# A two-layer backbone step: first products of two early feed-forward tiles taken ahead, and another rule for high priority

## The chip, the cores and the metric

The kernel runs on one core of a Trainium2 chip. The metric is the device time of one execution in microseconds, and what is given for a kernel is the median of its runs. The kernel before stands at 2413.62 us (three runs, 2412.04 to 2421.06).

## The reference

640 tokens (512 latent, 128 context) of width 1024 pass two layers. A layer is a half-step feed-forward, a mixer, and a second half-step feed-forward; each of the three is wrapped in an RMS normalisation before and after, with shift, scale and gate from a conditioning vector. The mixer is a two-dimensional Fourier transform between two projections in layer 0, and 16-head attention in layer 1.

```python
def _swiglu(h, w1, w2):
    gate, up = jnp.split(h @ w1, 2, axis=-1)      # D_FF = 2816
    return (jax.nn.silu(gate) * up) @ w2

def _half_ffn(x, m, k, g_pre, g_post, w1, w2):
    h = _modulated_prenorm(x, g_pre, m, k)
    return x + 0.5 * m[:, 3 * k + 2, None] * _rmsnorm(_swiglu(h, w1, w2), g_post)
```

## The kernel before, in words

**Sub-layers and halves.** The six sub-layers n = 0 to 5 are feed-forward, mixer, feed-forward, twice; 1 (Fourier) and 4 (attention) are mixers, 0, 2, 3 and 5 feed-forward. Activations lie with channels on the partitions, 8 chunks of 128 channels by 640 tokens, and the tokens are worked in two halves of 320. Everything is float32 with split operands: a number is a high part and a low part, and a product is three matmuls, high weight by high activation (L215), high weight by low activation (L216) and low weight by high activation (L217), in `mm3`. The high part of weights is an ACT copy (L198) and the low part a DVE subtraction (L200) in `send`; of activations L209 and L210 in `split`.

**The first projection of a feed-forward** has 22 tiles f of 128 hidden columns, each with a gate and an up column block. It runs a scheme with seven products in place of eight over the two halves of the tokens and the two halves of the channels. Of the activations B11, B12 (first four chunks, halves 0 and 1) and B21, B22 (last four) it needs T1 = B12 - B11, T2 = B22 - T1, T3 = B22 - B12 and T4 = T2 - B21, made in `combine` (L481, subtractions L491). Of the weights it needs, beside gate and up, the sums that `send` makes on DVE (L182 three times, L186 once) from two raw tiles; the units of weights are called "gate", "up", "sums" and "mix". Raw tiles come by DMA from SP (L161) into four buffers, the sums taking one of them; there are six high and six low weight buffers. `unit(i)` sends units up to three ahead of the one that is used.

**The start of a feed-forward.** `head` (L553) works half 0 alone: gate and up of tile 0 and gate of tiles 1 to 7, with B11 and B21, and keeps the sums in SBUF blocks of a ring of 20. `second` (L583) adds half 1 to tile 0: 24 matmuls with T1, then 24 with B22, then the adds L596, silu L579, product L580. `body(f)` (L599) runs a tile's other products; for tiles 1 to 7 these are mix by T1, sums by T2, sums by T3, up by T4 and, in `rest` (L639), mix by B22, with the DVE steps L615, L618, L627, L631, L632, L642 and L644 between. `w2` is the second projection in five slices (evicted on ACT at L677). `plan_ffn` (L699) writes down the order of these steps and of the weight units.

**Chains.** When a half of a sub-layer is done, `boundary` launches its `chain`: `post` normalises the output and adds it to the stream, `pre` normalises the stream for the next sub-layer (`inverse_rms` with small matmuls L430 and L438, a DVE step L432 and a POOL step L433 between; multiplications L462, scale and shift L468 and L470, then `split`, or `combine` for half 1 of a feed-forward). `tick` lets a chain go on by one step as matmuls are written. `step` gives a step of half 1 high priority, so that it goes ahead of other work that is ready on its engine, once half 0's own `post` is through (`self.normed[0][0]`).

## Time and profile before

| | before |
|---|---|
| median of three runs, us | 2413.62 (2412.04 to 2421.06) |
| the profiled execution, us | 2421.95 |
| its span, us | 2420.2 |
| mean granted TensorE clock | 0.986 |
| PE busy, us | 2325.5 (96%) |
| DVE busy, us | 1858.0 (77%) |
| ACT busy, us | 1256.2 (52%) |

The span goes from the first to the last instruction. Busy times are sums over an engine's instructions in the span; matmuls are pipelined, so that the length of one matmul in a timeline (0.31 us) is longer than the distance from one to the next. The granted clock is a share of full speed: 1.00 is the upper level, 0.50 the lower.

### The profile page before, as it was taken

What the parts mean: (1) busy time and instruction counts of PE and PEld (TensorE: products, weight loads), DVE (VectorE), ACT (ScalarE), POOL (GpSimd) and SP (SyncE); (2) the same over time, 40 slices, a digit from 0 to 9 for tenths busy, and PEclk for the clock granted to TensorE, in tenths of its full rate; (3) what the DMA queues carried; (4) which work ended last, traced back from release to release, by engine and by line L of the source; (5) the groups of instructions that cost most, each with busy time, mean ns of one, the idle gap of its engine ahead of it and who ended that gap; (6) DMA issues with size and microseconds to landing.
All of it is one profiled execution on the core that took longest, in us unless ns stands there. A gap on an engine that the chain in (4) does not pass through costs nothing.

```text
span 2420.2 us, 39323 instructions
## 1 busy us (share of the span) xinstructions
PE 2325.5 (96%) x15452; PEld 2239.1 (93%) x15452; DVE 1858.0 (77%) x3317; ACT 1256.2 (52%) x2405; POOL 72.5 (3%) x58
## 2 busy tenths in 40 slices
PE   6799999998999999999999999989999999999997
PEld 5799999997989999999899999987878898999997
DVE  7988888579788888858888887567777588675573
ACT  3554454564555554457555454744445574554544
POOL 3100000000000000000000000000000000000000
PEclk9899999999999999999999999999999999999999
DMA  6234544334424453443354353314334233332231
GB/s 255 86 123 123 174 124 125 136 94 142 143 87 146 125 168 116 137 147 114 97 157 133 121 168 119 127 56 125 123 107 129 64 112 97 95 99 66 81 124 60
DMA packets 84174, 291.77 MB, mean 121 GB/s; under 512 B 9234, under 2 KB 15634, under 8 KB 83988
## 3 DMA queue, kind: packets, MB, share of 16 engines
q1 hardware_dynamic: 83716, 288.93, 37.5%
q8 instruction: 121, 1.98, 0.3%
q14 instruction: 65, 0.53, 0.1%
q10 hardware_dynamic: 272, 0.33, 0.0%
HBM read 277.68 MB, written 11.53 MB: 120 GB/s over the span
## 4 chain that ended last, share of the span: by engine, by line
PE 75%; DVE 13%; DMA 5%; ACT 3%; issue 3%; POOL 0%; SPq 0%; DVEq 0%; ACTq 0%; POOLq 0%
PE main L215 21%; PE main L216 21%; PE main L217 21%; DMA raw<-in_w 4%; DVE lo L200 3%; DVE junk L358 3%; PE sum L1105 2%; PE score L215 2%; PE score L217 2%; PE score L216 2%; ACT hi L198 2%; DVE ring L210 1%; PE turn L1092 1%; PE score L1079 1%; DVE y L462 1%
## 5 line engine op out<-in xcount | busy, mean ns | idle before, releaser
L215 PE MATMUL main<-ring,hi 128*128 128x320 f32 x4032 | 1257.2, 314 | 35.6 <-ACT ring L209 19.0
L216 PE MATMUL main<-ring,hi 128*128 128x320 f32 x4032 | 1257.6, 312 | 7.9 <-DVE ring L210 7.5
L217 PE MATMUL main<-ring,lo 128*128 128x320 f32 x4032 | 1253.7, 312 | 7.8 <-DVE lo L200 6.0
L215 PEld LDWEIGHTS main<-ring,hi 128*128 128x128 f32 x4032 | 760.7, 189 | 52.4 <-ACT ring L209 22.8
L216 PEld LDWEIGHTS main<-ring,hi 128*128 128x128 f32 x4032 | 763.3, 189 | 15.1 <-DVE ring L210 11.3
L217 PEld LDWEIGHTS main<-ring,lo 128*128 128x128 f32 x4032 | 762.7, 189 | 11.9 <-DVE lo L200 6.8
L198 ACT ACTIVATE hi<-raw 128x1024 fp32r<-128x1024 f32 (+1 forms) x386 | 371.9, 966 | 511.9 <-PE main L216 342.1
L200 DVE TENSOR_TENSOR lo<-raw,hi 128x1024 fp32r<-128x1024 f32 (+1 forms) x380 | 419.1, 1103 | 145.5 <-ACT hi L198 142.7
L358 DVE SCALAR_TENSOR_TENSOR junk<-raw,wide 128x1024 bf16<-128x1024 f32 x256 | 312.2, 1220 | 15.0 <-DMA raw<-in_w_mod_t 11.9
L677 ACT ACTIVATE y<-main 128x320 f32<-128x320 f32 x320 | 136.7, 433 | 170.6 <-PE main L217 169.4
L665 ACT ACTIVATE main<-y 128x320 f32<-128x320 f32 x256 | 111.2, 439 | 41.1 <-DVE left L642 25.6
L394 DVE TENSOR_TENSOR total<-total,square 128x640 f32<-128x640 f32 x71 | 60.2, 853 | 86.4 <-ACT square L393 85.6
L200 DVE TENSOR_TENSOR lo<-sums,hi 128x1024 fp32r<-128x1024 f32 x84 | 102.5, 1221 | 22.1 <-ACT hi L198 21.8
L198 ACT ACTIVATE hi<-sums 128x1024 fp32r<-128x1024 f32 x84 | 88.8, 1057 | 36.9 <-PE main L216 18.2
L215 PE MATMUL score<-ring,hi 128*128 128x320 f32 x336 | 104.6, 311 | 1.2 <-ACT hi L198 1.2
L217 PE MATMUL score<-ring,lo 128*128 128x320 f32 x336 | 104.2, 310 | 0.0
L216 PE MATMUL score<-ring,hi 128*128 128x320 f32 x336 | 104.2, 310 | 0.0
L182 DVE TENSOR_TENSOR sums<-raw,raw 128x512 f32<-128x512 f32 x84 | 57.9, 689 | 40.1 <-DMA raw<-in_w 35.5
L433 POOL TENSOR_TENSOR col<-col,power 128x3 f32<-128x3 f32 x24 | 26.0, 1083 | 2081.7 <-DVE col L432 2081.7
L1094 ACT ACTIVATE right<-turn 128x384 f32<-128x384 f32 (+1 forms) x80 | 35.8, 448 | 84.3 <-PE turn L1092 83.9
L215 PEld LDWEIGHTS score<-ring,hi 128*128 128x128 f32 x336 | 63.5, 189 | 2.0 <-ACT hi L198 2.0
L618 DVE TENSOR_TENSOR left<-left,main 128x320 f32<-128x320 f32 x84 | 40.7, 485 | 30.8 <-PE main L217 29.8
(188 smaller groups left out, 2762.8 us busy)
## 6 DMA issues: line engine op xcount, KB each, us to landing
raw<-in_w SPq DMA_DIRECT2D x292, 512.0 KB, 3.6
raw<-in_w_mod_t SPq DMA_DIRECT2D x128, 512.0 KB, 3.8
raw<-in_qkv SPq DMA_DIRECT2D x26, 512.0 KB, 3.7
spill<-ring SPq DMA_DIRECT2D x12, 640.0 KB, 4.7
ring<-spill SPq DMA_DIRECT2D x12, 640.0 KB, 6.4
raw<-in_bias SPq DMA_DIRECT2D x16, 448.0 KB, 3.4
first<-in_w_mod_t SPq DMA_DIRECT2D x8, 512.0 KB, 10.2
raw<-in_four_in SPq DMA_DIRECT2D x8, 512.0 KB, 4.6
```

Source lines behind the costliest of these rows:

```text
L182: add = lambda out, a, b: nc.vector.tensor_tensor(out, a, b, op=ALU.add)
L198: nc.scalar.activation(hi, raw[:, at], AF.Copy)
L200: engine.tensor_tensor(lo, raw[:, at], hi.bitcast(F32), op=ALU.subtract)
L215: mm(out, whi, xhi, start=start, stop=False)
L216: mm(out, whi, xlo, start=False, stop=False)
L217: self.latest = mm(out, wlo, xhi, start=False, stop=stop)
L358: last = self.nc.vector.scalar_tensor_tensor(out=self.junk, in0=raw, scalar=1.0, in1=self.wide[:, cond, :], op0=ALU.mult, op1=ALU.mult, ac ...
L394: nc.vector.tensor_tensor(acc, acc, sq, op=ALU.add)
L618: tt(a, q, z, op=ALU.subtract)
L665: nc.scalar.activation(ps[:, :HALF], self.y[:, m, lo:hi], AF.Copy)
L677: nc.scalar.activation(self.y[:, m, lo:hi], ps[:, :HALF], AF.Copy)
L1105: nc.tensor.matmul(o, cache_v[:, ds] if k is None else v[:, k, ds], ptb[:, i * P + at : i * P + at + nq], start=n == 0, stop=n == len(tile ...
```

## The change

Four edits. (1) Of tiles 1 and 2 (`ACROSS`) the two mix products, by T1 and by B22, run right behind tile 0, in a new step `across`: both go into one PSUM bank, and ACT copies the bank to an SBUF block after each, so the copies hold mix by T1 and the sum of both; `body` and `rest` of these tiles read the copies in place of a bank. (2) `combine` splits B22 ahead of T2, T3 and T4, where it was last. (3) The weight units of tile 2 are listed so that its mix unit stands ahead of its sums; the order of the units comes out as before. (4) A step of half 1's chain has high priority if the chain leads into a feed-forward, from the start of the chain, and never if it leads into a mixer.

```diff
@@ -43,6 +43,7 @@
 PE_AT = (0, 2, 3, 5)
 SLICES = ((0, 2), (2, 6), (6, 11), (11, 16), (16, 22))
 EARLY = ((1, 2), (3, 4), (5, 6, 7))
+ACROSS = (1, 2)
 LATE = (NF - 2, NF - 1)
 BEHIND = (28, 20, 28, 28, 24, 0)
 BANKS = {"main": 4, "score": 2, "turn": 1, "sum": 1}
@@ -135,6 +136,7 @@
         self.normed = [[True, True], [True, True]]
         self.woven = []
         self.latest = None
+        self.hurry = False
         self.xs = {}
         self.hs = {n: Hidden(self.ring, n % 3 != 1) for n in range(DEPTH * 3)}
         self.fast = {}
@@ -229,7 +231,7 @@
 
     def step(self, half):
         due, gen = self.side[half]
-        with self.tc.high_priority() if half and self.normed[0][0] else ExitStack():
+        with self.tc.high_priority() if half and self.hurry else ExitStack():
             wait = next(gen, None)
         self.side[half] = None if wait is None else (max(due, 0) + wait, gen)
 
@@ -498,10 +500,10 @@
             put(1, h.steps[k][0], b12, b11)
         else:
             t1, t2 = h.steps[k]
+            self.split(h.at(0, c, 1, 2), h.at(1, c, 1, 2), b22)
             put(2, t2, b22, t1)
             put(3, t1, b22, b12)
             put(4, t2, t2, b21)
-            self.split(h.at(0, c, 1, 2), h.at(1, c, 1, 2), b22)
 
     def post(self, layer, sub, half, acc, last):
 
@@ -532,7 +534,7 @@
 
         nc = self.nc
         n = layer * 3 + 2 * which
-        g, kept = {}, {}
+        g, kept, crossed = {}, {}, {}
         h, high = self.h, self.tc.high_priority
         tt = nc.vector.tensor_tensor
 
@@ -596,15 +598,27 @@
                     tt(c, ps, c, op=ALU.add)
             gated(0, *kept[0], 1)
 
+        def across(f):
+
+            if "more" not in kept:
+                kept["more"] = self.ring(F32).rearrange("p (c t) -> p c t", c=4)
+            w = self.bank()[:, :HALF]
+            c = crossed[f] = [kept["more"][:, (f - 1) * 2 + i, :] for i in range(2)]
+            for i, x in enumerate((lambda k: h.sum(1, k), lambda k: h.chunk(4 + k, 1))):
+                product(w, f, "mix", 512 * i, x, not i)
+                with high():
+                    nc.scalar.activation(c[i], w, AF.Copy)
+
         def body(f):
             g[f] = self.ring(F32R).rearrange("p (a t) -> p a t", a=2)
             late, ready = f in LATE, f in kept
             x, y, z, w = (self.bank(kind)[:, :HALF] if want else None for kind, want in
-                          (("main", not ready), ("score", True), ("main", True), ("main", not late)))
+                          (("main", not ready), ("score", True), ("main", True), ("main", not late and f not in crossed)))
             q, a = (self.temp("left")[:, :HALF] for _ in range(2))
             if ready:
                 c1, s = kept[f]
-                product(w, f, "mix", 0, lambda k: h.sum(1, k), True)
+                if f not in crossed:
+                    product(w, f, "mix", 0, lambda k: h.sum(1, k), True)
             else:
                 c1, s = (self.temp("right")[:, :HALF] for _ in range(2))
                 product(x, f, "gate", 0, lambda k: h.chunk(k, 0), True)
@@ -624,7 +638,7 @@
                     nc.scalar.activation(s, x, AF.Silu)
             if not late:
                 with high():
-                    tt(a, a, w, op=ALU.add)
+                    tt(a, a, crossed[f][0] if f in crossed else w, op=ALU.add)
             v = self.temp("right")[:, :HALF]
             product(z, f, "up", 0, lambda k: h.sum(4, k), False)
             with high():
@@ -637,7 +651,10 @@
                 rest(f, w, q, a)
 
         def rest(f, w, q, a):
-            product(w, f, "mix", 512, lambda k: h.chunk(4 + k, 1), False)
+            if f in crossed:
+                w = crossed[f][1]
+            else:
+                product(w, f, "mix", 512, lambda k: h.chunk(4 + k, 1), False)
             with high():
                 nc.vector.scalar_tensor_tensor(out=q, in0=w, scalar=-1.0, in1=q, op0=ALU.mult, op1=ALU.subtract)
                 nc.scalar.activation(q, q, AF.Silu)
@@ -690,6 +707,8 @@
             elif op == "body":
                 self.finish(1)
                 body(a) if a else second()
+            elif op == "across":
+                across(a)
             elif op == "tail":
                 tail(a)
             elif op == "w2":
@@ -713,6 +732,8 @@
         due = 0
         for f in range(NF):
             plan.append(("body", f, None))
+            if f == 0:
+                plan += [("across", f, None) for f in ACROSS]
             if f == SLICES[due][1]:
                 plan += [("w2", (due, m), half) for m in range(NCH) for half in (0, 1)]
                 due += 1
@@ -734,9 +755,17 @@
             if op == "head":
                 for f in v:
                     unit("gate", f, 0)
+            elif op == "across":
+                unit("mix", v, 0, 1)
+                if v != ACROSS[-1]:
+                    unit("sums", v)
+                    unit("up", v)
             elif op == "body" and v:
+                if (v, "up") in self.w1_at:
+                    continue
                 if (v, "gate") in self.w1_at:
-                    unit("mix", v, 0, 1)
+                    if v not in ACROSS:
+                        unit("mix", v, 0, 1)
                     unit("sums", v)
                 else:
                     unit("gate", v, 0)
@@ -1168,7 +1197,8 @@
                 if not last:
                     yield from self.pre(*divmod(n + 1, 3), half, acc)
 
-            def boundary(half, acc, chain=chain):
+            def boundary(half, acc, chain=chain, n=n):
+                self.hurry = n % 3 != 0
                 self.launch(half, chain(half, acc), 2000)
 
             self.h = self.hs[n]
```

What moves on DVE at the start of the second feed-forward (sub-layer 2; the same holds at 3 and 5). In these rows `y`, `square` and `total` are activations of the chain and their sums, `ring` is a block that holds split parts or kept sums, `raw` and `sums` are weights. Lines of the changed kernel are two higher here than those of the kernel before (L210 is L212, L182 is L184, L186 is L188, L200 is L202, L596 is L598, L580 is L582). Before:

```order
L210 TENSOR_TENSOR ring_6875<-total_6782,ring_6874 128x640
L182 TENSOR_TENSOR sums_6800<-raw_6796,raw_6798 128x512
L210 TENSOR_TENSOR ring_6879<-y,ring_6878 128x640
L210 TENSOR_TENSOR ring_6875<-total_6828,ring_6874 128x640
L210 TENSOR_TENSOR ring_6879<-y,ring_6878 128x640
L182 TENSOR_TENSOR sums_6800<-sums_6800,raw_6798 128x512
L182 TENSOR_TENSOR raw_6796<-raw_6798 128x512
L596 TENSOR_TENSOR ring_6522<-main_6948,ring_6522 128x320
L186 SCALAR_TENSOR_TENSOR raw_6796<-raw_6796,sums_6800 128x512
L596 TENSOR_TENSOR ring_6522<-main_6949,ring_6522 128x320
L580 TENSOR_TENSOR right_7001<-ring_6522,left_7000 128x320
L200 TENSOR_TENSOR lo_6806<-raw_6796,hi_6805 128x1024
```

and with the change:

```order
L212 TENSOR_TENSOR ring_6869<-y,ring_6868 128x640 x2
...
L212 TENSOR_TENSOR ring_6884<-total_6787,ring_6883 128x640
L598 TENSOR_TENSOR ring_6527<-main_6953,ring_6527 128x320
L212 TENSOR_TENSOR ring_6884<-total_6833,ring_6883 128x640
L184 TENSOR_TENSOR sums_6805<-raw_6801,raw_6803 128x512
L598 TENSOR_TENSOR ring_6527<-main_6954,ring_6527 128x320
L184 TENSOR_TENSOR sums_6805<-sums_6805,raw_6803 128x512
L582 TENSOR_TENSOR right_7006<-ring_6527,left_7005 128x320
L184 TENSOR_TENSOR raw_6801<-raw_6803 128x512
L212 TENSOR_TENSOR ring_6692<-right_7006,ring_6692 128x320
L188 SCALAR_TENSOR_TENSOR raw_6801<-raw_6801,sums_6805 128x512
L202 TENSOR_TENSOR lo_6811<-raw_6801,hi_6810 128x1024
```

B22's two splits (`ring<-y`) stood third and fifth of the rows before; now both are in the first row, eleven rows ahead of the chain's last split. The weight sums, which stood partly inside the chain, all follow it, and tile 0's adds and product stand between them, ahead of the low weight that closes the piece.

On PE at the same place, the first matmul of each product, from tile 1's on. `ring` blocks name the activation: 6784 (6789 after) is T1, 6878 (6868) is B22, 6864 (6873) T2, 6869 (6878) T3, 6874 (6883) T4; `hi` 6805 (6810) are tile 1's mix weights, 6833 (6838) its sums. Before:

```order
L215 MATMUL main_7009<-ring_6784,hi_6805 128x320
...
L215 MATMUL score_7007<-ring_6864,hi_6833 128x320
...
L215 MATMUL main_7008<-ring_6869,hi_6833 128x320
...
L215 MATMUL main_7008<-ring_6874,hi_6850 128x320
...
L215 MATMUL main_7009<-ring_6878,hi_6805 128x320
```

and with the change:

```order
L217 MATMUL main_7012<-ring_6789,hi_6810 128x320
...
L217 MATMUL score_7094<-ring_6873,hi_6838 128x320
...
L217 MATMUL main_7012<-ring_6868,hi_6810 128x320
...
L217 MATMUL main_7052<-ring_6789,hi_7022 128x320
...
L217 MATMUL main_7095<-ring_6878,hi_6838 128x320
...
L217 MATMUL main_7052<-ring_6868,hi_7022 128x320
...
L217 MATMUL score_7148<-ring_6873,hi_7053 128x320
```

Tile 1's mix by B22, the last product of the tile before, comes third, and tile 2's mix weights (`hi_7022`) are used 36 rows behind the first of tile 1's.

On DVE at the start of attention, where half 1's chain meets the low parts of the v weights (`lo`); L462 is L464 there after, L468 is L470. Before:

```order
L200 TENSOR_TENSOR lo_15973<-raw_15970,hi_15972 128x1024
L462 TENSOR_TENSOR y<-ring_15363,rms_16208 128x2x320
...
L462 TENSOR_TENSOR y<-ring_15365,rms_16208 128x2x320
L468 TENSOR_SCALAR y<-y,coef 128x192 x4
L468 TENSOR_SCALAR y<-y,coef 128x128 x4
L200 TENSOR_TENSOR lo_16139<-raw_16136,hi_16138 128x1024
L210 TENSOR_TENSOR ring_15862<-y,ring_15861 128x2x320
```

and with the change:

```order
L202 TENSOR_TENSOR lo_15988<-raw_15985,hi_15987 128x1024
...
L464 TENSOR_TENSOR y<-ring_15378,rms_16223 128x2x320
L202 TENSOR_TENSOR lo_16154<-raw_16151,hi_16153 128x1024
L470 TENSOR_SCALAR y<-y,coef 128x192
L470 TENSOR_SCALAR y<-y,coef 128x128
L464 TENSOR_TENSOR y<-ring_15379,rms_16223 128x2x320
L464 TENSOR_TENSOR y<-ring_15380,rms_16223 128x2x320
L212 TENSOR_TENSOR ring_15855<-y,ring_15854 128x2x320
```

The second low part stood behind all of half 1's multiplications; now it stands behind one, and the first chunk's split behind a third of them.

On the chains into feed-forwards no row moves by the rule of priority.

## Rows read from the trace of the kernel before

**Rows 1.** The page, busy us of each engine, share of the span and instructions.
```profile
PE 2325.5 (96%) x15452; PEld 2239.1 (93%) x15452; DVE 1858.0 (77%) x3317; ACT 1256.2 (52%) x2405; POOL 72.5 (3%) x58
```
**Rows 2.** Stretches: us, then busy us and count of PE, PEld, DVE, ACT, POOL; clock; DMA.
```profile
240.00:300.00 60.00, 60.00 (x411) 60.00 (x410) 51.92 (x83) 29.96 (x55) 0.00 (x0) 1.00 0.56 173
705.20:750.10 44.90, 39.70 (x241) 38.27 (x241) 36.58 (x56) 21.71 (x38) 0.00 (x0) 0.92 0.32 96
709.00:712.00 3.00, 3.00 (x13) 3.00 (x13) 1.74 (x4) 0.00 (x0) 0.00 (x0) 0.50 0.00 0
722.20:750.10 27.90, 26.89 (x180) 26.53 (x181) 23.75 (x36) 16.98 (x31) 0.00 (x0) 1.00 0.40 117
1155.90:1196.40 40.50, 36.33 (x241) 35.05 (x240) 35.14 (x55) 20.81 (x37) 0.00 (x0) 1.00 0.33 104
2000.80:2043.10 42.30, 37.79 (x241) 36.58 (x239) 35.45 (x56) 20.79 (x37) 0.00 (x0) 0.96 0.32 100
1593.50:1618.00 24.50, 21.75 (x146) 21.34 (x145) 11.06 (x25) 8.46 (x18) 0.00 (x0) 0.93 0.14 44
```
**Rows 3.** Timeline of PE: start, us, operation, idle before it and releaser.
```profile
707.75 0.41 PE L216 MATMUL main<-ring,hi 128*128 128x320 f32 x1 [2.12 <-DVE ring L210]
...
713.87 0.41 PE L215 MATMUL main<-ring,hi 128*128 128x320 f32 x1 [1.10 <-ACT hi L198]
...
1158.01 0.42 PE L216 MATMUL main<-ring,hi 128*128 128x320 f32 x1 [1.72 <-DVE ring L210]
...
1162.89 0.42 PE L215 MATMUL main<-ring,hi 128*128 128x320 f32 x1 [1.39 <-ACT hi L198]
...
2003.26 0.41 PE L216 MATMUL main<-ring,hi 128*128 128x320 f32 x1 [2.06 <-DVE ring L210]
...
2008.14 0.42 PE L215 MATMUL main<-ring,hi 128*128 128x320 f32 x1 [1.39 <-ACT hi L198]
```
**Rows 4.** Timeline of DVE at the starts of sub-layers 2, 3 and 5.
```profile
708.35 0.81 DVE L210 TENSOR_TENSOR ring<-y,ring 128x640 fp32r<-128x640 f32 x1
709.09 0.68 DVE L182 TENSOR_TENSOR sums<-sums,raw 128x512 f32<-128x512 f32 x1
709.69 0.68 DVE L182 TENSOR_TENSOR raw<-raw 128x512 f32<-128x512 f32 x1
...
711.63 0.49 DVE L596 TENSOR_TENSOR ring<-main,ring 128x320 f32<-128x320 f32 x1 [1.26 <-PE main L217]
712.04 0.68 DVE L186 SCALAR_TENSOR_TENSOR raw<-raw,sums 128x512 f32<-128x512 f32 x1
...
1159.34 0.68 DVE L182 TENSOR_TENSOR sums<-sums,raw 128x512 f32<-128x512 f32 x1
...
2004.60 0.68 DVE L182 TENSOR_TENSOR sums<-sums,raw 128x512 f32<-128x512 f32 x1
```
**Rows 5.** Timeline of SP and ACT in sub-layer 2; groups and DMA issues of the page.
```profile
715.10 0.33 SPq L161 DMA_DIRECT2D raw<-in_w  x1
...
723.77 1.06 ACT L198 ACTIVATE hi<-raw 128x1024 fp32r<-128x1024 f32 x1 [8.13 <-DVE raw L186]
...
L677 ACT ACTIVATE y<-main 128x320 f32<-128x320 f32 x320 | 136.7, 433 | 170.6 <-PE main L217 169.4
...
raw<-in_w SPq DMA_DIRECT2D x292, 512.0 KB, 3.6
...
raw<-in_four_in SPq DMA_DIRECT2D x8, 512.0 KB, 4.6
```
**Rows 6.** Timelines of PE and DVE at the start of half 1 of attention.
```profile
1599.78 0.63 PE L215 MATMUL main<-ring,hi 128*128 128x320 f32 x1 [2.69 <-ACT ring L209]
...
1598.95 1.22 DVE L200 TENSOR_TENSOR lo<-raw,hi 128x1024 fp32r<-128x1024 f32 x1
```
**Rows 7.** Timeline of PE at the starts of sub-layers 0 and 1.
```profile
88.48 0.64 PE L215 MATMUL main<-ring,hi 128*128 128x320 f32 x1 [4.37 <-ACT ring L571]
...
538.41 0.70 PE L215 MATMUL main<-ring,hi 128*128 128x320 f32 x3 [1.31 <-ACT ring L209]
```

## The prediction, made before the changed kernel ran

> **What bounds the kernel now.** I read the busy table first: PE is busy for 2325.5 of 2420.2 us [rows 1]. The change neither adds nor removes a matmul, so only the 94.7 us in which PE stands still, and what a low clock costs behind such stands, can be won or lost. Next come stretches of PE, to price one matmul: 411 matmuls in 60.00 us, 0.146 us each, at granted clock 1.00, and 13 in 3.00 us at 0.50, the lower of the two levels (1.2 of 2.4 GHz) [rows 2]. Then the starts of the four feed-forward layers, where the change sits. I call them by sub-layer: 0, 2, 3 and 5. At 2, 3 and 5 the picture is the same. Tile 0's T1 products end, PE stands until B22's low part is there (2.12, 1.72 and 2.06 us, released by the DVE split L210), runs 24 matmuls, and stands once more until the weights of tile 1's "mix" are converted (1.10, 1.39 and 1.39 us, released by ACT L198) [rows 3]. From the end of the T1 products to tile 3's first matmul 240 or 241 matmuls take 44.90, 40.50 and 42.30 us [rows 2]; at 0.146 us each they would take 35.1. So 9.8, 5.4 and 7.2 us stand in these starts, 22.4 us together. No more than that can be won there.
>
> The readers should see why: DVE works without a break from the half's normalisation into the weight sums. In sub-layer 2 the last split starts at 708.35 and the next instruction at 709.09, with no idle time between [rows 4].
>
> **Part 1: B22's split goes ahead of T2, T3 and T4.** DVE issues as much as before, in another order. The two low parts of B22 stood at the end of ten DVE instructions; now they are five to six 128x640 operations of 0.74 us earlier (708.35 to 709.09 is one step [rows 4]). By then they are ready before the T1 products end, so the waits of 2.12, 1.72 and 2.06 us go [rows 3]. B22's 24 matmuls take 24 x 0.146 = 3.5 us, so tile 0 is done at about 708.7, 1159.4 and 2004.3.
>
> What is late next: tile 1's mix weights. In the changed order they stand on DVE behind the whole chain and more: tile 0's adds L596 (L598 after), its product L580 and its split are now ready early enough to go in between. The chain's last split ends at 709.09 less one weight sum that was in it (0.60) plus one add that now stands there (0.41, from 711.63 to 712.04): 708.9 [rows 4]. Behind it come three weight sums and the scalar_tensor_tensor L186, 4 x 0.61, and three tile operations, 3 x 0.41: 3.7 us, so 712.6. Before, L186 was through at 712.04 + 0.60 and the first mix matmul came at 713.87, 1.2 us later, the ACT conversion between [rows 3, 4]; so **713.8**, about as before. By the same steps sub-layer 3 gives 1159.34 - 0.60 + 0.41 + 3.7 + 1.2 = 1164.0 (1162.89 before) and sub-layer 5 2004.60 - 0.19 + 4.9 = 2009.3 (2008.14 before) [rows 3, 4]. The wait removed in front of B22 comes back in front of mix: one stand of some 5 us in place of two short ones.
>
> **Part 2: tiles 1 and 2 run T1 and B22 first.** The work is the same 216 matmuls from the first mix matmul to tile 3. But tile 2's mix weights are now wanted only 36 matmuls, 5.3 us, after tile 1's; before, they were wanted about 12 us after and waited for by nobody. Can they be there? Their second raw tile takes the buffer that the low part of mix 1 sets free: SP issues that load at 715.10, 1.2 us after the mix start at 713.87 [rows 3, 5]. It lands in 3.6 us by the median of 292 such loads [rows 5], then three sums and L186 take 2.45 us and the ACT conversion 1.06: 1.2 + 3.6 + 2.45 + 1.06 = 8.3 us after tile 1's first mix matmul. So PE stands up to **3.0 us** in front of tile 2's mix, a new wait; less if the clock is low in the 36 matmuls, since that only fills the stand. Behind it 180 matmuls remain, 26.3 us plus about 0.3 of small waits (180 took 26.89 busy of 27.90 before [rows 2]). I take 8.3 + 26.6 = 34.9 us from the first mix matmul to tile 3.
>
> Sub-layer 2: 713.8 + 34.9 = 748.7 against 750.1, **-1.4**. Sub-layer 3: 1164.0 + 34.9 = 1198.9 against 1196.4, **+2.5**. Sub-layer 5: 2009.3 + 34.9 = 2044.2 against 2043.1, **+1.1** [rows 2]. Together +2.2. No row before shows the stand in front of mix 2. Its lower bound is 0 (the load lands while PE still works, three starts better by 3.0 each, -6.8 together); its upper bound is a load of 4.6 us, as another kind of load of this size has [rows 5], 1.0 more each, +5.2 together. I take the median load, as 292 of them are of exactly this kind.
>
> Sub-layer 0 has the same edits, but PE waits 4.37 us there at 88.48 for a copy of tile 0's sums (L571) [rows 7], ahead of all that the change moves, and for nothing in the 45 us after it. I take 0, between -0.5 and +1.
>
> The sixteen ACT copies of 128x320 at about 0.43 us (the price of the L677 copies of that shape [rows 5]) lie in ACT's idle time: ACT stands 8.13 us ahead of the second mix conversion [rows 5]. If that cover went, each could hold a PSUM bank and cost PE its 0.43 us, 6.9 us together; with four main banks and two products open I take 0. One more ring block per layer is taken from a block already free, also 0.
>
> **Part 3: high priority.** The chains into feed-forward layers lose nothing and win nothing: their rows stand as before in the changed program. The chains into the mixers lose their priority. In attention that is visible: before, DVE runs all of half 1's multiplications (L462, then L468) ahead of the low part of the second v weight, which so starts at 1598.95, and only then the four splits; PE stands 2.69 us until 1599.78, for the ACT half (L209) of the split of half 1's first chunk, and that low part would have held it until 1600 as well [rows 6]. From 1593.5 to 1618.0, 24.50 us, PE runs 146 matmuls at clock 0.93 [rows 2]; 48 narrow ones of 0.117 and 96 of 0.147 at full clock are 5.6 + 14.1 = 19.7, so 4.8 us are lost in there. In the changed order the low part of that weight comes after a single L462, and one chunk is finished, split included, before the next. PE can run the 48 v matmuls through and starts half 1's 96 when the first chunk is there, at about 1599.7: 1599.7 + 14.1 = 1613.8 against 1618.0. I take **-4** (bounds 0 and -4.8). At the Fourier layer the wait of 1.31 us at 538.41 [rows 7] goes, but the two small matmuls of the normalisation now stand 4 matmuls apart rather than 16 with their DVE and POOL steps between, which costs PE about the same: 0, between -1.3 and +1.5.
>
> **The sum.** +2.2 + 0 - 4 + 0 = -1.8 us. The profiled execution took 2421.95 us; the median of the three shown is 2413.62, 8.3 us less, and the difference is carried over: **2411.8 us**. 0.5%, 12.1 us, is about what a measurement of this kernel can tell from no change.
>
> **Rivals.** *A, faster.* Mix 1 and mix 2 come in time, because DVE takes the weight sums in the gaps of the chain and the load lands early. Then the three B22 waits go unreplaced (2.12 + 1.72 + 2.06 = 5.9), with the low clock behind them (a clock of 0.92 over 44.90 us loses 3.6, one of 0.96 over 42.30 us 1.7 [rows 2]), and with attention -4: -15.2, **2398.4**. For it: DVE has idle time from 716 on. Against it: no DVE instruction leaves the stretch before mix 1, and DVE has no gap there [rows 4].
>
> *B, slower.* The stand before mix 2 lets the clock fall. The trace shows the fall after stands of 2.12 and 1.10 us in sub-layer 2 and none after 1.72 us in sub-layer 3 [rows 2, 3]. If each of the three new stands of 3 us is followed by a stretch as at 709 to 712, at 0.50, it costs what one cost in sub-layer 5, 1.7 us, that nothing hides, 5.1 for three; with loads 1.0 us longer, 3.0 more; and with nothing won in attention, where the low stretch moves ahead of half 1, 4 more. That is -1.8 + 5.1 + 3.0 + 4 = +10.3: **2423.9**. It decides by one thing: whether tile 2's mix conversion ends more than 6 us behind tile 1's first mix matmul. The Trainium skill, "TensorE: Matmul & The Clock Gate", section "Why this matters for your kernels", speaks against this change: it warns of long idle gaps between bursts of matmuls, because the engine then drops to its lower clock, and here two short stands are gathered into one long one. By that rule alone each of the gathered stands ahead of mix 1 is followed by a low stretch; that would cost nothing in my sum, where it lies in the stand that follows, and only the second stand's low stretch would move it, to about 2417. The trace bears it out in two of three starts.
>
> *C, the priority part does nothing.* The v tiles still wait for something else in attention (the conversion of the second v weight on ACT): the -4 goes, **2415.8**.
>
> **How the numbers follow.** Forecast 0.45, A 0.15, B 0.17, C 0.23. The range runs from A's time to just below B's: 2400 to 2422, which leaves out half of A and most of B's upper part, not 2 in 10. Faster by over 0.5% (below 2401.5) needs A nearly whole: 0.13. Slower by over 0.5% (above 2425.7) needs B and more: 0.05. Within: 0.82.
>
> **What would show it.** Right: no PE wait released by DVE L210 (L212 after) at the three starts; one PE wait of 4 to 5 us before the first mix matmul, and one of 1.5 to 3 us before tile 2's, both released by ACT's weight conversion; in attention no PE wait at half 1's start and clock near 1.00. Wrong: no wait before tile 2's mix (then A), a clock of 0.50 behind it and a longer stretch to tile 3 than 35 us (B), or attention's stretch still at 24 us (C).

## The result, and the profile after

The changed kernel takes **2422.43 us** (median of 20 runs, 2420.66 to 2426.11), the kernel before 2417.57 us over 20 runs of its own (2412.04 to 2421.87; the 2413.62 shown ahead was the median of the first three). The ratio is 1.0024 with a 95% interval of 1.0017 to 1.0030: slower by 0.24%, a small difference, but clear of zero. A change of -1.8 us was forecast; it came to +4.9 us. Of the 10.6 us between the forecast time, 2411.8, and the measured one, 6.7 are this difference, and 4.0 are the kernel before, whose median over 20 runs lies that much above the one over three.

Nothing of the loss stands on the page of the profile: its profiled execution (2420.66 us, span 2418.9) differs by a fraction of a per cent in every engine.

```profile
PE 2323.1 (96%) x15452; PEld 2235.6 (92%) x15452; DVE 1855.9 (77%) x3317; ACT 1264.0 (52%) x2421; POOL 72.7 (3%) x58
```

The waits of PE tell more. Here is its timeline, with the columns of [rows 3], at the starts of sub-layers 2, 3 and 5 (line L217 is L215 of before) and, at 1585.50, in attention:

```profile
711.49 0.64 PE L217 MATMUL main<-ring,hi 128*128 128x320 f32 x1 [4.89 <-ACT hi L200]
...
720.29 0.42 PE L217 MATMUL main<-ring,hi 128*128 128x320 f32 x1 [0.59 <-ACT hi L200]
...
1160.98 0.63 PE L217 MATMUL main<-ring,hi 128*128 128x320 f32 x1 [4.51 <-ACT hi L200]
...
1170.26 0.41 PE L217 MATMUL main<-ring,hi 128*128 128x320 f32 x1 [0.59 <-ACT hi L200]
...
1585.50 0.55 PE L217 MATMUL main<-hi,ring 128*128 128x256 f32 x1 [5.07 <-DVE ring L985]
...
2006.62 0.63 PE L217 MATMUL main<-ring,hi 128*128 128x320 f32 x1 [4.82 <-ACT hi L200]
...
2015.38 0.42 PE L217 MATMUL main<-ring,hi 128*128 128x320 f32 x1 [1.02 <-ACT hi L200]
```

The waits for L210 in [rows 3] are gone. In front of the first mix matmul PE now stands once, for 4.89, 4.51 and 4.82 us. A second stand comes in front of tile 2's mix, 0.59, 0.59 and 1.02 us. In attention the wait of [rows 6] at half 1's start is gone too, but the one ahead of it has grown to 5.07 us; in the trace before it was 3.59 us:

```profile
1583.99 0.55 PE L215 MATMUL main<-hi,ring 128*128 128x256 f32 x1 [3.59 <-DVE ring L956]
```

Stretches, with the columns of [rows 2]: the whole start of sub-layer 2 from the end of T1 to tile 3, the piece behind the stand, the start of sub-layer 3, and half 1 of attention:

```profile
703.20:748.00 44.80, 38.92 (x242) 37.42 (x241) 35.13 (x56) 22.60 (x42) 0.00 (x0) 0.92 0.31 95
...
711.40:717.40 6.00, 5.86 (x22) 5.47 (x23) 3.88 (x5) 1.95 (x4) 0.00 (x0) 0.54 0.52 148
...
1153.90:1199.20 45.30, 39.13 (x240) 37.64 (x239) 34.80 (x55) 23.31 (x43) 0.00 (x0) 0.92 0.33 97
...
1592.50:1614.70 22.20, 22.06 (x163) 21.84 (x163) 12.06 (x25) 9.48 (x16) 0.85 (x1) 1.00 0.16 49
```

Behind the stand the clock is near 0.50 (0.54 over 6 us). Attention's stretch of 163 matmuls takes 22.20 us at 1.00. The 24.50 us of [rows 2] hold 146 matmuls; for the same 163 the kernel before took 26.30 us in its first profile:

```profile
1590.20:1616.50 26.30, 23.55 (x163) 23.14 (x163) 13.08 (x31) 8.43 (x15) 0.85 (x1) 0.94 0.13 40
```

Counted matmul by matmul from the end of T1 to tile 3's first one, the three starts take 44.8, 45.6 and 44.4 us; [rows 2] show 44.9, 40.5 and 42.3.

### The profile page after: what moved, and what is told of

It reads as the page before. It is cut to its first block, busy times and chain, and to the rows that moved or that the text cites. A ratio compares the mean times of both kernels' runs of the same rounds, so it can differ in the third digit from the quotient of the medians.

```text
span 2418.9 us, 39332 instructions
## 1 busy us (share of the span) xinstructions
PE 2323.1 (96%) x15452; PEld 2235.6 (92%) x15452; DVE 1855.9 (77%) x3317; ACT 1264.0 (52%) x2421; POOL 72.7 (3%) x58
## 4 chain that ended last, share of the span: by engine, by line
PE 76%; DVE 13%; DMA 5%; ACT 3%; issue 2%; POOL 0%; SPq 0%; DVEq 0%; ACTq 0%; POOLq 0%
PE main L217 22%; PE main L218 21%; PE main L219 21%; DMA raw<-in_w 4%; DVE lo L202 3%; PE sum L1134 2%; DVE junk L360 2%; PE score L217 2%; PE score L219 2%; PE score L218 2%; DVE ring L212 2%; ACT hi L200 2%; PE turn L1121 1%; PE score L1108 1%; DVE sums L184 1%
## 5 line engine op out<-in xcount | busy, mean ns | idle before, releaser
L217 PE MATMUL main<-ring,hi 128*128 128x320 f32 x4032 | 1259.1, 314 | 41.1 <-ACT hi L200 16.4
L217 PEld LDWEIGHTS main<-ring,hi 128*128 128x128 f32 x4032 | 760.7, 189 | 59.7 <-ACT ring L211 18.2
L200 ACT ACTIVATE hi<-raw 128x1024 fp32r<-128x1024 f32 (+1 forms) x386 | 371.9, 966 | 483.8 <-PE main L218 334.2
L202 DVE TENSOR_TENSOR lo<-raw,hi 128x1024 fp32r<-128x1024 f32 (+1 forms) x380 | 419.2, 1104 | 148.2 <-ACT hi L200 145.8
L202 DVE TENSOR_TENSOR lo<-sums,hi 128x1024 fp32r<-128x1024 f32 x84 | 102.6, 1221 | 24.0 <-ACT hi L200 23.9
L200 ACT ACTIVATE hi<-sums 128x1024 fp32r<-128x1024 f32 x84 | 88.9, 1058 | 34.5 <-PE main L218 22.2
L217 PE MATMUL score<-ring,hi 128*128 128x320 f32 x336 | 105.1, 313 | 0.1
L184 DVE TENSOR_TENSOR sums<-raw,raw 128x512 f32<-128x512 f32 x84 | 57.9, 690 | 43.8 <-DMA raw<-in_w 38.6
L632 DVE TENSOR_TENSOR left<-left,main 128x320 f32<-128x320 f32 x84 | 40.7, 485 | 36.1 <-PE main L219 35.6
L217 PEld LDWEIGHTS score<-ring,hi 128*128 128x128 f32 x336 | 63.7, 189 | 1.3 <-ACT hi L200 1.3
```

The source lines that it names most:

```text
L184: add = lambda out, a, b: nc.vector.tensor_tensor(out, a, b, op=ALU.add)
L200: nc.scalar.activation(hi, raw[:, at], AF.Copy)
L202: engine.tensor_tensor(lo, raw[:, at], hi.bitcast(F32), op=ALU.subtract)
L217: mm(out, whi, xhi, start=start, stop=False)
```

## The experiments

Every kernel was timed beside the kernel before on the same chip. The kernel before took 2416.68 to 2418.48 us in these groups, so kernels of different groups are compared by their ratios; the intervals of two ratios that are close often overlap. "Matmuls at half speed" are counted from the starts in the trace: those that follow the one ahead by 0.23 to 0.33 us, where 0.147 is the distance at full clock, among the 60 from the first mix matmul on.

| kernel | us | ratio to before | 95% interval |
|---|---|---|---|
| changed kernel | 2422.43 | 1.0024 | 1.0017 to 1.0030 |
| changed kernel, again | 2423.76 | 1.0018 | 1.0009 to 1.0027 |
| before, again | 2418.55 | 1.0003 | 0.9994 to 1.0012 |
| split first | 2422.28 | 1.0021 | 1.0013 to 1.0030 |
| priority | 2413.47 | 0.9987 | 0.9978 to 0.9997 |
| products ahead only | 2424.03 | 1.0036 | 1.0022 to 1.0049 |
| tile 1 alone ahead | 2417.80 | 0.9997 | 0.9988 to 1.0005 |
| filler | 2425.38 | 1.0031 | 1.0019 to 1.0043 |
| split first, filler | 2419.77 | 1.0010 | 1.0001 to 1.0019 |
| tile 1 alone, filler | 2415.29 | 0.9988 | 0.9980 to 0.9996 |
| fifth raw buffer | 2415.04 | 0.9986 | 0.9978 to 0.9995 |
| sums early | 2420.08 | 1.0012 | 1.0002 to 1.0022 |
| sums early, nothing ahead | 2412.00 | 0.9975 | 0.9965 to 0.9984 |
| sums behind B22, nothing ahead | 2412.22 | 0.9981 | 0.9972 to 0.9990 |
| sums behind B22, tiles 1, 2 | 2415.61 | 0.9995 | 0.9986 to 1.0004 |
| sums behind B22, tile 1 | 2404.79 | 0.9945 | 0.9933 to 0.9958 |

**Before, again.** No edit.

> The kernel before, unchanged, to see what differs from one profiled execution to the next. My theory: the profiled execution shown before (2421.95 us) was a slow one because it had three stretches at the lower clock that stand in stages which the change does not touch (near 504, 1147 and 1268 us, 1.5 us each); they fall by chance, so they will be missing here or stand elsewhere, and the profiled execution will be about 2417 us. Rival: they belong to the kernel; they stand at the same three places again and the profiled execution takes about 2422 us. The timed ratio is 1.000 within 0.001 either way.

The profiled execution took 2412.42 us, 9.5 less than the first one, with nothing changed. 3.3 us of that lie in the start of sub-layer 2, which now takes

```profile
701.50:743.50 42.00, 37.04 (x245) 35.59 (x244) 36.80 (x56) 21.92 (x39) 0.00 (x0) 1.00 0.34 103
```

at a clock of 1.00, where [rows 2] show 44.90 us for nearly the same matmuls at 0.92. Matmul by matmul it is 41.6 against 44.9. Another 2.3 us lie in attention, whose stretch at half 1's start takes 24.80 us here, with no low clock in it:

```profile
1583.00:1607.80 24.80, 22.05 (x162) 21.64 (x161) 12.32 (x28) 9.09 (x16) 0.45 (x1) 1.00 0.14 44
```

Another 1.5 us lie near 504 us, where the first profile had a low clock and this one has none. The stretch at 1147 is the same in both, so it belongs to the kernel, and 1268 gave 0.9 us back, not 1.5; neither was at a low clock. The theory holds in its main point and not in its list: single profiled executions of this kernel differ by up to 10 us, most of it in low clocks that come in one execution and not in the next. Sub-layer 2's start and attention's were two of them, and the prediction had taken them for the rule.

**Each part alone.**

```diff
             t1, t2 = h.steps[k]
+            self.split(h.at(0, c, 1, 2), h.at(1, c, 1, 2), b22)
             put(2, t2, b22, t1)
             put(3, t1, b22, b12)
             put(4, t2, t2, b21)
-            self.split(h.at(0, c, 1, 2), h.at(1, c, 1, 2), b22)
```

> Only B22's split ahead of T2 to T4. Theory (the wait moves): the three PE waits of 2.1, 1.7 and 2.1 us for L210 go, the wait before the first mix matmul grows from 1.1 to 1.4 us to 4 to 5 us at each of the three starts, and with the weight sums later by about 0.2 to 1 us the time is 0 to 3 us longer than before. Rival (the split is the good part, the early products the bad one): 4 to 6 us shorter than before.

Measured: 0.21% slower. The waits for L210 went and PE stood 4.89, 4.51 and 4.8 us before mix 1; 15, 19 and 7 matmuls ran at half speed behind it. The theory said 0 to 3 us, it was some 5. The edit that was meant to take a wait away is by itself one of the two that cost time.

```diff
-        with self.tc.high_priority() if half and self.normed[0][0] else ExitStack():
+        with self.tc.high_priority() if half and self.hurry else ExitStack():
...
```

(`hurry` is set as in the change.)

> Only the other rule of high priority. Theory: attention's start wins 2.8 us as in the changed kernel, nothing else moves: 2 to 3.5 us shorter than before. Rival (the priority of the chain into feed-forwards from its first step does the harm): 3 to 5 us longer than before, with the loss in sub-layers 2 and 5 or in the mixers' ends.

Measured: 0.13% faster, as forecast (about 3 us, interval 0.5 to 5). At the Fourier layer, from 526 to 540 us, 1.1 us are won (0.9 to 1.1 in every profile with the new rule). In attention, matmul by matmul against the undisturbed second profile of the kernel before, the piece with half 1's start takes 2.7 us less, and the piece ahead of it 1.5 us more, since this stand comes 1.5 us longer than before (the same row as in the changed kernel):

```profile
1579.89 0.55 PE L216 MATMUL main<-hi,ring 128*128 128x256 f32 x1 [5.07 <-DVE ring L957]
```

The third kernel keeps the old place of B22's split and the old priority, and has `across` and its unit order alone.

> Only the early products of tiles 1 and 2 with their copies in SBUF. Theory: B22 and mix 1 are waited for as before, and in front of tile 2's mix a new wait of 0.6 to 1.5 us comes at each start: 2 to 4 us longer than before. Rival (the early products fill the stands): 2 us or more shorter than before. Second rival (the copies hold up PE): over 6 us longer.

Measured: 0.36% slower, 5 to 12 us by the interval: more than the theory's 2 to 4 us, and about what the second rival gave (over 6). The waits for B22 and mix 1 are those of [rows 3] within 0.5 us, and a stand of 2.3 to 2.7 us comes before tile 2's mix, with 18 or 19 matmuls at half speed in the 60 at all three starts, where before had 2 to 15. No wait for the copies shows at these starts, and matmul by matmul they take 4.6, 3.8 and 2.4 us more than in the second profile of the kernel before, so the stand and the clock are the loss, not the copies that this rival named.

**Which tile's products cost.** `ACROSS = (1,)` in the changed kernel:

> The changed kernel with tile 1 alone taken ahead. Theory: the wait before tile 2's mix (0.5 to 1.2 us) and the later one for tile 2's first sums go, the stand of 4.7 to 5.0 us before mix 1 and the low clock behind it stay: 1 to 3 us shorter than the changed kernel, and still 1 to 3 us longer than the kernel before. Rival (tile 2's early products are the loss): 5 us or more shorter than the changed kernel, so shorter than the kernel before.

Measured: 2417.80, as fast as before (0.9988 to 1.0005). Against both tiles it is 4.6 us faster by the medians and 0.27%, some 6.5 us, by the ratios: beyond the theory (1 to 3), and at the rival's place (5 or more), though not faster than before. Tile 2's products ahead cost time; that tile 1's pay is not shown by this run.

**A fifth raw buffer.** `NRAW = 5`, `NBLK = 19` in the changed kernel:

> The changed kernel with a fifth raw weight buffer, and 19 ring blocks instead of 20 to make room for it. Theory (tile 2's mix waits for the raw buffer that mix 1 sets free): the load of tile 2's second raw tile leaves 5 us or more sooner, the stands before tile 2's mix (0.8, 0.8 and 1.2 us) go, the stand of 4.7 to 5.0 us before mix 1 stays; but without a stand to hide in, the low clock then costs in full: 0 to 3 us shorter than the changed kernel. Rival (DVE's order holds up tile 2's sums, not the load): the stands before tile 2's mix stay as they are.

Measured: 0.14% faster than before, and 0.38% faster than the changed kernel (7.4 us by the medians). Both theories missed part of it. In sub-layer 2 the load goes out at 706.66 rather than 712.72, and the program itself moved: with a free buffer the weight sums of tile 1 stand ahead of the chain's multiplications on DVE. The stand before mix 1 is gone there, and the one before tile 2's mix is 3.60 us:

```profile
706.66 1.33 SPq L163 DMA_DIRECT2D raw<-in_w  x2
...
711.97 0.63 PE L217 MATMUL main<-ring,hi 128*128 128x320 f32 x1 [3.60 <-ACT hi L200]
```

In sub-layer 3 one of 3.5 us remains before mix 1, in sub-layer 5 one of 2.8 before mix 1 and one of 2.9 before mix 2. So the buffer does bind, through the load and through the order in which DVE gets to the weights; how much is due to each, and what one ring block less does, was not timed alone.

**The clock.** The next three kernels fill the stand before mix 1 with 24 matmuls whose result nobody reads; no weight and no DVE step moves.

```diff
+            if f == 1 and n:
+                fill = self.bank("turn")[:, :HALF]
+                x0 = h.chunk(4, 1)
+                for i in range(24):
+                    nc.tensor.matmul(fill, x0[0][:, :P], x0[0], start=i == 0, stop=i == 23)
```

> The changed kernel with 24 matmuls that nobody reads (B22 by itself, into a spare PSUM bank) between tile 0 and the first mix product of sub-layers 2, 3 and 5. They take 3.5 us of a stand of 4.7 to 5.0 us and delay nothing. Theory (the low clock behind the gathered stand is the larger part of the loss): the 17 to 25 matmuls that run at half speed behind it go, 2 to 3 us at each of the three starts, less what the stand before tile 2's mix takes back: 3 to 7 us shorter than the changed kernel, 2415 to 2419 us. Rival (the stands themselves are the loss, whatever the clock): the same time as the changed kernel, 2422 us.

Measured: 2425.38, not shorter: 3 us longer by the medians, 0.07% by the ratios, whose intervals overlap. Sub-layer 3 shows why, by the stands that are left:

```profile
1164.19 0.42 PE L217 MATMUL main<-ring,hi 128*128 128x320 f32 x1 [1.00 <-ACT hi L200]
...
1173.21 0.64 PE L217 MATMUL main<-ring,hi 128*128 128x320 f32 x1 [2.59 <-ACT hi L200]
```

The clock stayed up through mix 1, PE reached tile 2's mix sooner, and stood there 2.59 us for the same weights. Behind that stand the clock fell, where nothing hides it, and so it did in sub-layer 5; in sub-layer 2 it fell ahead of tile 2's mix in spite of the fill. At each start 16 to 18 matmuls still ran at half speed. With the low clock before it, the stand had been 0.59 us. So in the changed kernel the end of these 36 matmuls is set by tile 2's weights, as the prediction had it, and the low clock in them costs next to nothing (9.3 us for them in sub-layer 3 without the fill, 9.0 with it).

> B22's split first alone, with 24 matmuls that nobody reads in the gathered stand ahead of mix 1 of sub-layers 2, 3 and 5 (3.5 of 4.7 to 5.0 us). Here no stand before tile 2's mix follows in which a low clock could hide. Theory (the low clock behind the gathered stand made B22's split a loss): the 10 to 21 matmuls at half speed behind the stand fall to about 5, 1 to 2 us at each start: 3 to 6 us shorter than the split alone, 2416 to 2419 us. Rival (the clock is not the cause; the weight sums' later place is): 0 to 1 us shorter than the split alone, 2421 to 2422 us.

> The changed kernel with tile 1 alone taken ahead, and the same 24 matmuls in the same place. Theory: 3 to 6 us shorter than without them, 2412 to 2415 us. Rival: no change, 2417 to 2418 us.

Without tile 2's products ahead there is no second stand, and the fill seems to pay: 0.11% less for the split alone, 0.09% less for tile 1 alone, about 2.5 us in each, a little under the 3 to 6 forecast. The intervals of each pair overlap at their ends; that both go the same way, and what the clock does, is the evidence. For sub-layer 3, the split alone, PE at the first mix matmul and the stretch behind it:

```profile
1161.61 0.64 PE L215 MATMUL main<-ring,hi 128*128 128x320 f32 x1 [4.51 <-ACT hi L198]
...
1161.00:1170.50 9.50, 8.60 (x36) 7.93 (x36) 6.25 (x9) 2.26 (x4) 0.00 (x0) 0.64 0.39 110
```

and with the fill:

```profile
1164.20 0.41 PE L215 MATMUL main<-ring,hi 128*128 128x320 f32 x1 [0.99 <-ACT hi L198]
...
1163.00:1172.00 9.00, 6.95 (x44) 6.24 (x43) 6.29 (x11) 2.53 (x3) 0.00 (x0) 1.00 0.37 117
```

36 matmuls in 9.50 us at 0.64, and 44 in 9.00 us at 1.00; the 36 from the first mix matmul on take 9.3 us without the fill and 6.9 with it. In sub-layers 3 and 5 the matmuls at half speed went from 19 and 7 to 2 and 2; in sub-layer 2 there are still 14. So, as far as 2.5 us with such an interval tells, about half of what the split costs is the clock behind the gathered stand, and the rest the later weights (mix 1 starts 8.6, 8.2 and 8.5 us after the end of T1, before in an undisturbed execution 7.5, 7.1 and 7.4).

**The changed kernel, again.**

> The changed kernel, unchanged, for a second profile. Theory: the stands before mix 1 are 4.7 to 5.1 us again at the three starts with 15 or more matmuls at half speed behind each, and those before tile 2's mix 0.5 to 1.3 us; the low stretches elsewhere (near 1147 and 1268 us) may come or go. Rival: the low stretches behind mix 1 come by chance too, and one or more is missing here.

Stands of 4.88, 4.50 and 4.82 us, with 19, 22 and 13 matmuls at half speed; in the first profile 18, 22 and 14. The low clock behind the gathered stand comes every time, unlike the one in sub-layer 2 of before.

**Another place for tile 1's weight sums.** In the changed kernel the last split of the chain starts at 705.90, and the three weight sums and L188 of tile 1 come from 706.63 on; their raw tiles had landed at 691 us. DVE's rows, with SP's load of tile 2's raw tile, the sums of that tile and its conversion on ACT:

```profile
705.90 0.82 DVE L212 TENSOR_TENSOR ring<-total,ring 128x640 fp32r<-128x640 f32 x1
...
709.66 0.68 DVE L188 SCALAR_TENSOR_TENSOR raw<-raw,sums 128x512 f32<-128x512 f32 x1
...
712.72 0.33 SPq L163 DMA_DIRECT2D raw<-in_w  x1
...
716.45 0.69 DVE L184 TENSOR_TENSOR sums<-raw,raw 128x512 f32<-128x512 f32 x1 [2.02 <-DMA raw<-in_w]
...
718.39 0.69 DVE L188 SCALAR_TENSOR_TENSOR raw<-raw,sums 128x512 f32<-128x512 f32 x1
...
719.19 1.05 ACT L200 ACTIVATE hi<-raw 128x1024 fp32r<-128x1024 f32 x1
```

The load goes out 1.2 us after mix 1's first matmul, DVE waits 2.02 us for it, and the conversion ends at 720.25: 8.8 us after that matmul, where the prediction had 8.3. First edit: the sums and the split of tile 1's mix at high priority.

```diff
+            with self.tc.high_priority() if key[1] in (1,) else ExitStack():
                 add(sums[:, one], gate[:, one], up[:, one])
...
+        with self.tc.high_priority() if kind == "mix" and key[1] in (1,) else ExitStack():
             nc.scalar.activation(hi, raw[:, at], AF.Copy)
```

> The changed kernel with tile 1's weight sums, and the split of its mix weights, at high priority, so that DVE makes them between the chain's multiplications: their raw tiles landed at 691 us in sub-layer 2 and waited for DVE until 706.6. Theory (what binds is DVE's order, not its amount of work): the stand of 4.7 to 5.0 us before mix 1 shrinks to 1 to 2 us for the low part, T1 and B22 come 2.4 us later, which the half-0 products still cover; but tile 2's mix is now wanted sooner and stands 2 to 4 us: 4 to 9 us shorter than the changed kernel. Rival (DVE's amount of work binds: what is put ahead pushes T1 and B22 behind the point where PE needs them): the stand moves in front of T1, no gain over the changed kernel.

> The kernel before with B22's split first, the other rule of priority and tile 1's weight sums at high priority, but no product taken ahead. Theory: as with the products taken ahead, without the stand before tile 2's mix, since 12 us lie between the two: at each of sub-layers 2, 3 and 5 the stands shrink from 5.7 us to 2, with no low clock, and attention keeps its 2.8: 8 to 15 us shorter than the kernel before, 2402 to 2409 us. Rival (DVE's amount of work binds): 0 to 3 us shorter than before, from attention alone.

Measured: 2420.08 and 2412.00. With the products ahead it gains 2 to 3 us on the changed kernel, less than forecast and with overlapping intervals: of the stands in it, those before tile 2's mix are 2.4 to 2.6 us. Without them it lies 0.25% under before, some 6 us, short of the 8 to 15 forecast. In front of mix 1 at most 0.5 us is left, for its low part, and part of the gain is lost ahead of it, as the rival had it: T1 comes late (sub-layer 2):

```profile
703.00 0.56 PE L218 MATMUL main<-ring,hi 128*128 128x320 f32 x2 [2.29 <-ACT ring L212]
```

Second edit: the sums are written inside the chain, right behind B22's split, so that T1 and B22 keep their place and T2 to T4 wait.

```diff
             self.split(h.at(0, c, 1, 2), h.at(1, c, 1, 2), b22)
+            if c == 6 and self.units[self.sent][0] == "mix" and self.units[self.sent][1][1] == 1:
+                self.held = False
+                self.unit(self.sent, 0)
+                self.held = True
             put(2, t2, b22, t1)
```

(`unit` now stops ahead of tile 1's mix unit of sub-layers 2, 3 and 5 while `held` is set.)

> The kernel before with B22's split first, the other rule of priority, and tile 1's weight sums written right behind B22's split in the chain of sub-layers 2, 3 and 5, so ahead of the second T2, T3 and T4. Theory (in the kernel with the sums at high priority from the start, T1 came 2 to 3 us late, as the stand of 2.3 us in front of it shows; what binds is where the sums stand among the chain's operations): T1 and B22 on time, mix weights on time, stands of 1 to 3 us at each start in place of 5.7, no gathered stand, so no low clock: 10 to 16 us shorter than the kernel before, 2402 to 2408 us. Rival (the wait only moves on, now before T2 to T4): within 3 us of the kernel with the sums at high priority, 2409 to 2414 us.

> The same place for tile 1's weight sums, in the changed kernel with tiles 1 and 2 taken ahead. Theory: now the products taken ahead have their weights and give T2 to T4 3.5 us more, and the buffer of tile 2's second raw tile comes free 5 us sooner, so tile 2's mix is waited for by at most 1 us: as fast as the version without them or up to 4 us faster, 2400 to 2407 us. Rival (products of two tiles ahead still want weights sooner than DVE and the loads give them): 3 to 6 us slower than the version without them.

> The same with tile 1 alone taken ahead. Theory: the best of the three, since it gives T2 to T4 more time and asks nothing of tile 2's weights: 2400 to 2406 us. Rival (taking ahead gives nothing, the place of the sums all): the same as the version without products taken ahead, within 1 us.

Measured: 2412.22, 2415.61 and 2404.79. With nothing ahead the rival is right: PE stands once, for the low part of tile 1's sums, which T2 needs, and the clock falls behind it (the stretch from that matmul on):

```profile
714.62 0.64 PE L222 MATMUL score<-ring,lo 128*128 128x320 f32 x1 [3.22 <-DVE lo L205]
...
714.60:720.00 5.40, 5.02 (x23) 4.75 (x24) 4.95 (x9) 1.53 (x2) 0.00 (x0) 0.71 0.32 97
```

With both tiles ahead the low part of the sums is waited for, and tile 2's mix again; 3.4 us more than without products ahead is what the rival gave:

```profile
712.19 0.42 PE L223 MATMUL score<-ring,lo 128*128 128x320 f32 x1 [1.45 <-DVE lo L206]
...
717.42 0.41 PE L221 MATMUL main<-ring,hi 128*128 128x320 f32 x1 [3.49 <-ACT hi L204]
```

With tile 1 alone, T1's and B22's products of tile 1 cover that time, and no stand is longer than 1.47 us:

```profile
714.70 0.41 PE L223 MATMUL score<-ring,lo 128*128 128x320 f32 x1 [1.46 <-DVE lo L206]
...
718.64 0.42 PE L221 MATMUL main<-ring,hi 128*128 128x320 f32 x1 [0.74 <-DVE left L640]
...
714.70:721.70 7.00, 5.94 (x37) 5.40 (x38) 6.27 (x11) 2.48 (x4) 0.00 (x0) 1.00 0.27 75
...
1158.00:1165.00 7.00, 5.87 (x36) 5.32 (x37) 6.28 (x12) 2.39 (x3) 0.00 (x0) 1.00 0.22 77
```

The clock is 1.00 behind them in both sub-layers. On DVE the four sums now stand between the splits, from 699.22 to 704.6, and the low part follows at 706.04, 0.8 us behind the end of T1, where the split alone had it 8.6 us behind:

```profile
699.22 0.68 DVE L188 TENSOR_TENSOR sums<-raw,raw 128x512 f32<-128x512 f32 x1
...
703.97 0.68 DVE L192 SCALAR_TENSOR_TENSOR raw<-raw,sums 128x512 f32<-128x512 f32 x1
...
706.04 1.22 DVE L206 TENSOR_TENSOR lo<-raw,hi 128x1024 fp32r<-128x1024 f32 x1
```

This kernel takes **2404.79 us** (five runs), 0.55% less than before (0.42 to 0.67) and 0.8% less than the changed kernel. It differs from tile 1 alone only in the place of the weight sums: that is worth 0.52%. From the kernel with nothing ahead it differs only in tile 1's products: they are worth 0.36% here. It keeps the new place of B22's split, the new priority and the early products of tile 1, leaves tile 2 as it was, and moves the weight sums.

## Why the prediction was wrong

**What was right.** The waits for B22 went. The stand before mix 1 was worked out as 5 us and came as 4.5 to 4.9; from the end of T1 to the first mix matmul the sum gave 8.6, 8.1 and 8.5 us and the trace shows 8.57, 8.19 and 8.51. The wait in front of tile 2's mix is there, and for the reason given: the load that waits for mix 1's raw buffer. It is 0.6 to 1.0 us and not 3.0, because the low clock fills the time before it, as the forecast had allowed. The chains into feed-forwards cost nothing by their priority, and attention's half 1 starts without its wait. The Fourier layer, put at 0 between -1.3 and +1.5, gave 1.1 us.

**Where it failed**, by its terms:

1. *"34.9 us from the first mix matmul to tile 3."* It came to 36.2, 37.4 and 35.9 us, 4.8 us more over the three starts. Tile 2's weights are there 8.8, 9.3 and 8.8 us behind tile 1's first mix matmul, not 8.3: load, sums and conversion each came 0.1 to 0.2 us later than their price. In sub-layer 3 another 0.5 us is the price of a copy that the prediction had put at 0. L188 is through at 1168.61, but ahead of the conversion (L200) ACT has the second of the new copies (L610), and that waits for mix 1's last matmul on PE, which the low clock made late:

```profile
1167.92 0.69 DVE L188 SCALAR_TENSOR_TENSOR raw<-raw,sums 128x512 f32<-128x512 f32 x1
...
1168.83 0.44 ACT L610 ACTIVATE ring<-main 128x320 f32<-128x320 f32 x1 [2.86 <-PE main L219]
1169.16 1.05 ACT L200 ACTIVATE hi<-raw 128x1024 fp32r<-128x1024 f32 x1
```

The 180 matmuls behind take 27.2 to 28.1 us, not 26.6; 0.1 to 1.0 us of that is a stand for the DVE step L632, where the sum had put 0.3 for all small waits.
2. *The baseline of sub-layer 2.* The sum set 748.7 against 750.1 and booked -1.4. The 44.90 us of [rows 2] were an execution with two low stretches; in the second profile of the kernel before the same matmuls take 41.6 us. Against that, the changed kernel's 44.8 is +3.2. The kernel with the new priority alone has the same start, and its profile had one low stretch there and 43.8 us. Whether that one profile stood for the rule was never asked, though the three runs shown spread over 9 us.
3. *"The difference is carried over."* For the same reason the distance of 8.3 us from the profiled execution to the median was no constant; over 20 runs it is 4.4. Nor does a measurement need 0.5% to tell a change: the interval of the ratio is 0.13% wide.
4. *Attention, -4.* The 24.50 us it was worked out from held a low stretch that the second profile does not have. Against that one half 1's piece won 2.7 us, and the stand ahead of it, 3.59 us in the trace before, grew by 1.5, which the prediction had left out of its price: -1.2. With the 1.1 us of the Fourier layer that is 2.3 us, where the new rule, timed alone, gives 0.13%, about 3.
5. *Sub-layer 0, 0.* It costs 1.0 us in the first profile and 2.0 in the second, 33.4 and 34.4 us for a piece that takes 32.45 before, with a stand of 0.5 and 1.2 us in it.

Terms 1, 2, 4 and 5 come to some 11 us over the forecast, where the medians show 6.7. They are counted against the second profile of the kernel before, 2412.42 us, and the median of that kernel, 2417.57, lies 5.2 above it; how often each low stretch comes in the timed runs is not known.

Rival B was the nearest: its place, the weights of tile 2, is where the time went, and its point of decision, more than 6 us, was passed; but the forecast's own 8.3 us passes it as well, so that it could not tell the two apart. Its price of +10.3 was twice what came: the loads took 0.1 to 0.2 us longer and not 1.0, attention did win, and the low clock fell ahead of the second stand, not behind it. The forecast had seen that hiding and was right on it, as the fill in the changed kernel shows.

The rule of the Trainium skill, "TensorE: Matmul & The Clock Gate", section "Why this matters for your kernels", that long idle gaps between bursts of matmuls bring back the lower clock, is borne out here: behind the stands of 4.5 to 4.9 us the clock fell at all three starts of four profiles (the changed kernel twice, the split alone, tile 1 alone; 7 to 22 matmuls at half speed), and filling them left 2 to 5 at two starts of three. For the split alone the fill is worth about 2.5 us of 5. That the clock also fell behind some stands of 1.5 us (last section) goes beyond that rule. The rule does not price the changed kernel, where the weights of tile 2 are later than the slow matmuls.

In sum, by ratios: the split +0.21%, the priority -0.13%, tile 1's products -0.11% (tile 1 alone against those two, if the parts add up) and tile 2's +0.27%. The timed ones have intervals of about 0.1% to either side and the differences wider ones, so tile 1's share is not clear of zero. Nor is it shown that parts add up: split, priority and both tiles' products, each timed alone, give +0.21, -0.13 and +0.36%, +0.44% together (about 0.2% to either side), against +0.24% for the whole. A loss in one part can hide in another, as the low clock behind the first stand hides ahead of the second.

## What to carry to other kernels

When a wait on an engine that works without a break is taken away, ask what now stands last on that engine: here B22's split went ahead and the weight sums became the last, and most was won by moving those sums, with as much work to cover them as one tile gives (0.52%). Taking work ahead also takes its operands ahead: tile 2's products were wanted 3.5 to 4 us before raw buffer, load, sums and conversion could give their weights. Before a stretch is used as the baseline of a sum, look whether its low clock is there in a second execution.

## What the runs showed of the hardware

The same program, run again, had a start of 41.6 us at clock 1.00 where it had had 44.9 at 0.92, with the same stand of 2.1 us before B22 in it. In sub-layer 5 of the kernel before the clock fell in both executions, behind stands of 2.06, 1.39 and 0.39 us that end within 6 us of one another; in sub-layer 2, with nearly the same stands, in one of two; in sub-layer 3, with 1.72, 1.39 and 0.38, in neither.

Single short stands do the same. Behind those of 1.46 and 1.47 us at the best kernel's three starts the clock did not fall; behind one of 1.48 in the same execution, with PE at work all the while before it, it did:

```profile
502.92 0.86 PE L221 MATMUL main<-ring,hi 128*128 128x320 f32 x4 [1.48 <-ACT ring L215]
...
505.00:508.00 3.00, 3.00 (x13) 3.00 (x13) 3.00 (x5) 3.00 (x8) 0.00 (x0) 0.50 0.37 97
```

In the kernel before that same stand was followed by a low clock in one execution of two. Counted over all seventeen profiles, three such single stands of 1.4 to 1.5 us (near 503, 1110 and 1560 us) had one begin during the stand or within 4 us behind it in 13 of 51 cases. Of the 37 stands of 3.2 to 5.1 us between 92 and 2385 us every one had.

So short stands can make this kernel's time scatter, and long ones bring the low clock every time. The 110 timed executions of the kernel before beside the experiments agree: the nine with a mean clock of 0.991 took 2413.7 us on average, the sixteen with 0.986 took 2420.6. The best kernel's five runs lie within 2.5 us (2403.12 to 2405.58), the 26 of the kernel before beside it within 11.4; but five runs are few.
